# The recurrence's key tile without zero padding, multiplied as four 64x64 quarters

## The chip, the cores and the metric

One core of a Trainium2 chip runs the whole program. The metric is the device time of one execution in microseconds (us). The engines are TensorE (PE in the rows; PEld is its weight load), VectorE (DVE), ScalarE (ACT), GpSimd (POOL) and SyncE (SP), which here issues every DMA. Each takes its instructions in order from its own queue.

## The reference, cut to what matters

The program is one transformer layer on 2048 latent and 256 context tokens in float32: adaLN, a mixer of two head groups, and a gated MLP with a convolution. One head group is a bidirectional RWKV-7 recurrence of 8 heads of 64 channels, run forward and backward over the tokens:

```python
def step(S, inp):
    r_t, w_t, k_t, v_t, kk_t, b_t = inp
    sa = jnp.einsum('bhvk,bhk->bhv', S, kk_t)
    S = (S * w_t[:, :, None, :] - sa[..., None] * b_t[:, :, None, :]
         + v_t[..., None] * k_t[:, :, None, :])
    return S, jnp.einsum('bhvk,bhk->bhv', S, r_t)
```

The kernel computes it in chunks of 64 tokens. Inside a chunk the recurrence becomes products of the chunk's keys with its queries, the inverse of a triangular 64x64 matrix, and a few small matmuls that carry the state S from chunk to chunk.

## The kernel before

There are four phases, one after the other with some overlap: the input projection (phase 1, to about 945 us), the recurrence (phase 2b, about 945 to 1570 us), the attention of the other head group, and the output projection with the MLP.

**Phase 1** makes, besides other things, the key pairs of the recurrence. `prep` (40 calls: 4 head pairs, 5 blocks of tokens, 2 directions) builds a tile G of 128 partitions (two heads of 64 channels) by chunks by 128 columns. The columns of one chunk hold the two kinds of key, e = 0 and e = 1, of 64 tokens each. DVE finishes G (L530), and one DMA of SP (L531) stores it in the scratch tensor `pd`.

**Phase 2b** has 36 steps; step i handles one chunk of the forward and one of the backward direction (d = 0, 1), four head pairs each, so 8 units. Three pieces of work belong to it.

- `stage_g` (L1011 to L1035) multiplies keys by queries. `load` (L978) brings a 512 KB tile QP and the keys PK. PK has two halves: n = 0 holds the 64x64 blocks that stay on the block diagonal (head f, rows f and columns f), n = 1 those off it (rows f, columns 1-f), and the rest of both halves is zero, set once by POOL (L969). Four DMAs of 128 KB (L987) fill the blocks. For each d and n, L1018 makes four 128x128 matmuls into one PSUM bank `pa`. The n = 0 bank goes to AP by ACT (L1020), the n = 1 bank to ST by DVE in two half-height masked multiplies (L1026). POOL adds the two halves of PK to a dense tile PD (L1028, once per d), and PE transposes PD (L1033) for `tok`. ACT also copies QP into ST (L1024).
- `extract` and `invert`: ACT cuts the triangles out of AP (L1041), POOL masks them (L1042), and for two steps together (a pair) DVE transposes them (L1050), runs 31 rounds of two dependent small operations (L1056, L1057, 62 operations in all), and transposes the result twice (L1060, L1061).
- `assemble` and `chain`: the state update. PE forms Z (L1118), ACT copies the half of d = 0 and DVE that of d = 1 (L1120, Zk), PE multiplies by the inverse (L1133), ACT scales (L1135), PE multiplies by tok (L1142), DVE adds to the state S (L1143, once per d), and POOL scales it into X for the next step (L1146, L1147).

The three PSUM banks named `pa` rotate among L1018, L1033 and the two products of `assemble` (L1079, L1090). The order on each engine comes from a scheduler which weighs priorities that `boosted` sets for each piece; it interleaves several steps, and its order is what the order rows below show.

Of the kernel before, what the change touches and what calls it, by code (L numbers as in the profile page):

```python
# [8 lines left out]
F32 = mybir.dt.float32  # L9
# [3 lines left out]
ALU = mybir.AluOpType  # L13
# [4 lines left out]
P = 128  # L18
# [10 lines left out]
CH = 64  # L29
# [168 lines left out]
def phase1(tc, I, T, pr, ident, bones, keep):  # L198
    nc = tc.nc
    with ExitStack() as st:  # L200
# [3 lines left out]
        hp = rpool(st, "hT", 1)  # L204
# [101 lines left out]
        with ExitStack() as s2:  # L306
# [3 lines left out]
            pv = rpool(s2, "psv", 1, space=PSUM)  # L310
# [131 lines left out]
        with ExitStack() as s3:  # L442
# [50 lines left out]
            def prep(h, b, O, K):  # L493
                t0, n = BLOCKS[b]
                m = n // CH
                rr = K
                if b:
                    rr = cp.tile([P, BLK], F32, name="rr", bufs=2)
                    nc.sync.dma_start(out=rr, in_=T["rwT"][h * P:(h + 1) * P, t0:t0 + n])
                for d in range(2):  # L500
                    i0 = t0 // CH
                    if d:
                        i0 = 0 if b == 0 else 36 + 4 - i0 - m

                    def v(ap):
                        ap = ap[:, 0:n]
                        return ap[:, ::-1] if d else ap

                    def c(ap):
                        return ap[:, 0:n].rearrange("p (m t) -> p m t", t=CH)  # L510

                    t = []
                    for e in range(2):
                        z = pv.tile([P, BLK], F32, name="pk")
                        nc.tensor.matmul(z[:, 0:n], lhsT=W4[:, d, e, h * P:(h + 1) * P], rhs=los[b][:, e], start=True, stop=True)
                        t.append(cp.tile([P, BLK], F32, name="t%d" % e, bufs=2))
                        nc.scalar.activation(out=t[e][:, 0:n], in_=v(z), func=AF.Tanh, scale=0.5)
                    sg, ta = t
                    nc.gpsimd.tensor_scalar(out=sg[:, 0:n], in0=sg[:, 0:n], scalar1=0.5, scalar2=0.5, op0=ALU.mult, op1=ALU.add)
                    cs = cp.tile([P, BLK], F32, name="cs", bufs=2)  # L520
                    nc.vector.tensor_tensor_scan(out=cs[:, 0:n], data0=smask[:, 0:n], data1=sg[:, 0:n], initial=0.0, op0=ALU.mult, op1=ALU.add)
                    nc.scalar.activation(out=sg[:, 0:n], in_=cs[:, 0:n], func=AF.Exp, scale=-CDEC)
                    nc.scalar.activation(out=cs[:, 0:n], in_=cs[:, 0:n], func=AF.Exp, scale=CDEC)
                    W, IW = c(sg), c(cs)
                    nc.vector.tensor_copy(out=pr.wc[:, i0:i0 + m, d, h], in_=W[:, :, CH - 1])
                    G = cp.tile([P, 2 * BLK], F32, name="G", bufs=2)[:, 0:2 * n].rearrange("p (m e t) -> p m e t", e=2, t=CH)
                    nc.vector.scalar_tensor_tensor(out=G[:, :, 0], in0=c(ta), scalar=1.0, in1=c(v(K)), op0=ALU.add, op1=ALU.mult)
                    nc.scalar.activation(out=ta[:, 0:n], in_=ta[:, 0:n], func=AF.Identity, scale=hka[:, h:h + 1], bias=oka[:, h:h + 1])
                    nc.gpsimd.tensor_tensor(out=G[:, :, 1], in0=c(v(O)), in1=c(ta), op=ALU.mult)
                    nc.vector.tensor_tensor(out=G, in0=G, in1=IW.unsqueeze(2).broadcast_to([P, m, 2, CH]), op=ALU.mult)  # L530
                    nc.sync.dma_start(out=T["pd"][d * 4 + h, :, i0 * P:(i0 + m) * P], in_=G.rearrange("p m e t -> p (m e t)"))  # L531
                    Q = cp.tile([P, 2 * BLK], F32, name="Q", bufs=2)[:, 0:2 * n].rearrange("p (m t) -> p m t", t=P)
                    nc.gpsimd.tensor_tensor(out=Q[:, :, 1:CH], in0=c(v(K))[:, :, 1:CH], in1=W[:, :, 0:CH - 1], op=ALU.mult)
                    nc.scalar.copy(out=Q[:, :, 0:1], in_=c(v(K))[:, :, 0:1])
                    nc.gpsimd.tensor_tensor(out=Q[:, :, CH:P], in0=c(v(rr)), in1=W, op=ALU.mult)
                    nc.sync.dma_start(out=T["qd"][d * 4 + h, :, i0 * P:(i0 + m) * P], in_=Q.rearrange("p m t -> p (m t)"))
# [161 lines left out]
G = 3  # L698
# [243 lines left out]
CH = 64  # L942
# [4 lines left out]
def phase2b(tc, I, T, pr, ident):  # L947
# [17 lines left out]
        return ivx[1 if p >= 2 and p % 2 == 0 else 0]  # L965

    def pk_tiles(p, n):
        PK = p.tile([P, 2, 8, P], F32, name="PK%d" % n)
        nc.gpsimd.memset(PK, 0.0)  # L969
        PKs.append((p.tile([P, 8, P], F32, name="QP%d" % n), PK))  # L970

    order = [list(range(NS)), list(range(3, -1, -1)) + list(range(NS - 1, 3, -1))]
    bts, ivs, PKs = {}, [], []
    Ls, Bs = {}, {}
    qv = T["qd"].rearrange("u p (i t) -> i p u t", t=P)
    pv = T["pd"].rearrange("u p (i n t) -> i n p u t", n=2, t=CH)

    def load(i):  # L978
        if i >= NS or i in Ls:
            return  # L980
        QP, PK = PKs[1 if i >= 4 and i % 2 == 0 else 0]
        nc.sync.dma_start(out=QP, in_=qv[i])
        for n in range(2):
            for f in range(2):
                s = slice(f * 64, f * 64 + 64)
                o = (f ^ n) * 64
                nc.sync.dma_start(out=PK[s, n, :, o:o + 64], in_=pv[i, n, s])  # L987
        Ls[i] = QP, PK

    hd = lpool("rgen")  # L990
    gm = hd.tile([P, 2, P], F32, name="gm")
    adm = hd.tile([P, 32], F32, name="adm")
    PD = hd.tile([P, 8, P], F32, name="PD")
    pk_tiles(hd, 0)
    load(0)
    nc.sync.dma_start(out=gm, in_=I["gmask"].rearrange("p (a b) -> p a b", a=2))
# [11 lines left out]
    def psa():  # L1008
        return pam.tile([P, 4, P], F32, name="pa")

    def stage_g(i, B):  # L1011
        QP, PK = Ls.pop(i)
        for d in range(2):
            u = slice(d * 4, d * 4 + 4)
            for n in range(2):
                g = psa()
                for hp in range(4):
                    nc.tensor.matmul(g[:, hp], lhsT=PK[:, n, d * 4 + hp], rhs=QP[:, d * 4 + hp], start=True, stop=True)  # L1018
                if n == 0:
                    nc.scalar.copy(out=B["AP"][:, u], in_=g)  # L1020
                for f in range(2):
                    s, o = slice(f * 64, f * 64 + 64), slice((1 - f) * 64, (1 - f) * 64 + 64)
                    if n == 0:
                        nc.scalar.copy(out=B["ST"][s, u, f], in_=QP[s, u])  # L1024
                    else:
                        nc.vector.tensor_tensor(out=B["ST"][o, u, f], in0=g[o], in1=gm[o, 1:2].broadcast_to([64, 4, P]), op=ALU.mult)  # L1026
                yield
            nc.gpsimd.tensor_tensor(out=PD[:, u], in0=PK[:, 0, u], in1=PK[:, 1, u], op=ALU.add)  # L1028
        nc.gpsimd.tensor_tensor(out=B["AP"][:, :, CH:P], in0=B["AP"][:, :, CH:P], in1=gm[:, 1:2, CH:P].broadcast_to([P, 8, CH]), op=ALU.mult)
        for d in range(2):  # L1030
            g = psa()
            for hp in range(4):
                nc.tensor.transpose(out=g[:, hp], in_=PD[:, d * 4 + hp], identity=ident)  # L1033
            nc.scalar.copy(out=B["tok"][:, d * 4:d * 4 + 4], in_=g)
            yield  # L1035

# [843 lines left out]
```

## Time and profile before

| | |
|---|---|
| median of 3 runs | 4146.94 us |
| lowest, highest | 4144.19, 4151.88 us |
| span of the profiled execution | 4140.8 us |
| PE busy, share of span | 3824.6 us, 92% |
| DVE busy | 2671.8 us, 65% |
| ACT, POOL busy | 1881.5, 1543.3 us |

The span is that of the instructions in one profiled execution; the median lies 6.1 us above it. A share over the whole span mixes phases: outside the recurrence PE works on matmuls of 512 columns nearly without a gap, so the phase of the change has to be read by itself.

### The profile page before, as it was taken

Reading aid. Unit: us, or ns where it says so; the run is one execution under the profiler, and the core shown is the slowest. Engines: PE = TensorE matmul, PEld = TensorE weight load, DVE = VectorE, ACT = ScalarE, POOL = GpSimd, SP = SyncE. Lnnn points to the kernel's source line nnn. Section 1 sums busy time; section 2 is a strip of 40 time slices with the busy share of each in tenths; the row PEclk is TensorE's granted clock in tenths of the full one; section 3 lists DMA queues with packets and bytes.
Section 4 is the critical chain, followed back from the end, with each engine's and each line's share of the span. In section 5 each row is a group of like instructions: output and inputs, shape, how many; then the busy total and the mean of one; then the engine's idle time right before and its main releaser. Section 6 shows DMA issues by size and latency. Waiting matters only on the chain. (4 is left out here: it accounts for less than half of the span.)

```text
span 4140.8 us, 65493 instructions
## 1 busy us (share of the span) xinstructions
PE 3824.6 (92%) x25471; PEld 3213.6 (78%) x25471; DVE 2671.8 (65%) x3869; ACT 1881.5 (45%) x3678; POOL 1543.3 (37%) x1617
## 2 busy tenths in 40 slices
PE   7998888897899987989999899899999999999999
PEld 4777666676888876888898778788888888878887
DVE  3467678978889886888989868754444444420243
ACT  4235454466666656777777644521112112221211
POOL 3237467844444433455444366511101101022222
PEclk8999999998999988999999999999999999999999
DMA  4554546554434333020102163311111111131333
GB/s 174 160 168 154 162 146 214 205 161 94 97 95 101 94 85 101 8 61 22 33 6 74 51 219 136 117 61 51 46 43 62 46 41 56 51 101 44 115 114 102
DMA packets 464724, 400.80 MB, mean 97 GB/s; under 512 B 131613, under 2 KB 393702, under 8 KB 463390
## 3 DMA queue, kind: packets, MB, share of 16 engines
q1 hardware_dynamic: 464414, 396.61, 31.3%
q8 instruction: 201, 3.29, 0.3%
q14 instruction: 109, 0.89, 0.1%
HBM read 269.51 MB, written 131.74 MB: 97 GB/s over the span
## 5 line engine op out<-in xcount | busy, mean ns | idle before, releaser
L36 PE MATMUL o<-h2H,wuL 128*128 128x512 f32 x1920 | 761.7, 397 | 0.8 <-POOL wuL L1586 0.8
L34 PE MATMUL o<-h2H,wuH 128*128 128x512 f32 x1920 | 755.5, 394 | 5.6 <-DVE h2H L179 3.7
L35 PE MATMUL o<-h2L,wuH 128*128 128x512 f32 x1920 | 759.1, 395 | 0.2 <-DVE h2L L180 0.2
L1586 POOL TENSOR_TENSOR wuL<-wuraw,wuH 128x1024 fp32r<-128x1024 f32 x76 | 182.2, 2399 | 871.0 <-ACT wuH L1585 871.0
L34 PEld LDWEIGHTS o<-h2H,wuH 128*128 128x128 f32 x1920 | 362.0, 189 | 90.8 <-DVE h2H L179 3.9
L35 PEld LDWEIGHTS o<-h2L,wuH 128*128 128x128 f32 x1920 | 361.9, 189 | 89.9 <-DVE h2L L180 1.6
L36 PEld LDWEIGHTS o<-h2H,wuL 128*128 128x128 f32 x1920 | 362.1, 189 | 83.5 <-POOL wuL L1586 1.5
L34 PE MATMUL mm<-hH,wH 128*128 128x512 f32 (+1 forms) x968 | 384.5, 398 | 23.1 <-DVE hH L179 13.0
L787 DVE TENSOR_REDUCE nb<-S 128x1 f32<-128x768 f32 x384 | 357.8, 948 | 54.1 <-PE S L786 52.8
L35 PE MATMUL mm<-hL,wH 128*128 128x512 f32 (+1 forms) x968 | 382.0, 395 | 1.0 <-DVE rstd L162 0.9
L788 ACT ACTIVATE P<-S,nb 128x768 f32<-128x768 f32 x384 | 345.8, 907 | 77.4 <-DVE nb L787 74.5
L36 PE MATMUL mm<-hH,wL 128*128 128x512 f32 (+1 forms) x968 | 380.9, 394 | 0.0
L1617 DVE TENSOR_SCALAR co<-cs,cols 128x1024 f32<-128x1024 f32 x88 | 139.8, 1590 | 314.4 <-ACT cs L1606 313.0
L785 PE MATMUL S<-kH,qs 128*128 128x384 f32 x768 | 293.4, 382 | 36.1 <-ACT P L788 33.8
L829 PE MATMUL pv<-V,aT 128*128 128x128 f32 x2304 | 310.0, 279 | 5.5 <-DVE O L845 3.0
L1606 ACT COPY cs<-o 128x512 f32<-128x512 f32 x176 | 103.0, 586 | 449.8 <-PE o L36 449.6
L829 PEld LDWEIGHTS pv<-V,aT 128*128 128x128 f32 x2304 | 286.6, 195 | 9.1 <-DVE O L845 5.8
L786 PE MATMUL S<-kL,qs 128*128 128x384 f32 x768 | 261.2, 340 | 0.0
L815 DVE SCALAR_TENSOR_TENSOR P<-P,f,P 128x768 f32<-128x768 f32 x192 | 243.9, 1283 | 12.5 <-POOL P L813 10.9
L34 PEld LDWEIGHTS mm<-hH,wH 128*128 128x128 f32 x968 | 191.1, 198 | 63.8 <-DVE hH L179 13.9
L35 PEld LDWEIGHTS mm<-hL,wH 128*128 128x128 f32 x968 | 191.5, 198 | 40.2 <-DVE hL L180 2.2
L36 PEld LDWEIGHTS mm<-hH,wL 128*128 128x128 f32 x968 | 191.4, 198 | 38.9 <-issue 0.7
(362 smaller groups left out, 8103.6 us busy)
## 6 DMA issues: line engine op xcount, KB each, us to landing
wraw<-in_w_in_dram SPq DMA_DIRECT2D x52, 512.0 KB
wuraw<-in_w_up_dram SPq DMA_DIRECT2D x44, 512.0 KB
scr_actT<-co SPq DMA_DIRECT2D x44, 512.0 KB
QP<-scr_qd SPq DMA_DIRECT2D x36, 512.0 KB
PK<-scr_pd SPq DMA_DIRECT2D x144, 128.0 KB
mww<-in_w_mod_dram SPq DMA_DIRECT2D x64, 256.0 KB
scr_pd<-G SPq DMA_DIRECT2D x32, 512.0 KB
scr_qd<-Q SPq DMA_DIRECT2D x32, 512.0 KB
```

The lines of the kernel that those rows point to most:

```text
L34: nc.tensor.matmul(out, lhsT=lH, rhs=rH, start=first, stop=False)
L35: nc.tensor.matmul(out, lhsT=lH, rhs=rL, start=False, stop=False)
L36: nc.tensor.matmul(out, lhsT=lL, rhs=rH, start=False, stop=last)
L785: nc.tensor.matmul(S[:, b, 0:HB], lhsT=qs[:, qt * P:(qt + 1) * P], rhs=kH[:, sl], start=True, stop=False)
L786: nc.tensor.matmul(S[:, b, 0:HB], lhsT=qs[:, qt * P:(qt + 1) * P], rhs=kL[:, sl], start=False, stop=True)
L787: nc.vector.tensor_reduce(out=nb[:, m, g:g + 1], in_=S[:, :, 0:HB], op=ALU.max, axis=AX.XY, negate=True)
L788: nc.scalar.activation(out=Pm[m][:, g * GW:(g + 1) * GW].rearrange("p (b x) -> p b x", b=2), in_=S[:, :, 0:HB], func=AF.Exp, bias=nb[:, m, ...
L815: nc.vector.scalar_tensor_tensor(out=Pm[0][:, sls[g - 1]], in0=Pm[0][:, sls[g - 1]], scalar=f[:, 0, g - 1:g], in1=Pm[1][:, sls[g - 1]], op ...
L829: nc.tensor.matmul(pv, lhsT=aT[:, j], rhs=V[:, k0 + j], start=(k0 + j == 0), stop=(k0 + j == KTT - 1))
L1586: eng.tensor_tensor(out=L, in0=raw, in1=H.bitcast(F32), op=ALU.subtract)
L1606: nc.scalar.copy(out=S[:, 1 + b * BLK:1 + (b + 1) * BLK], in_=o)
L1617: nc.vector.tensor_scalar(out=O, in0=S[:, t0:t0 + 1024], scalar1=w[0], scalar2=None, op0=ALU.mult)
```

## The change

The keys are stored so that one 128x128 tile per unit is already what PD was. `prep` writes the partitions of head 0 as they are and those of head 1 with the two kinds of key exchanged, so one DMA becomes three. `load` brings PK with one DMA. PK has no zero half and no memset; PD and its POOL addition are gone, and the transposes read PK. Each 128x128 product of n = 0 and n = 1 becomes two 64x64 quarters (64 rows, 64 columns of weights, 128 columns moving); the diagonal ones write bank `g`, the others bank `go`, both asked for at once.

```diff
-                    nc.sync.dma_start(out=T["pd"][d * 4 + h, :, i0 * P:(i0 + m) * P], in_=G.rearrange("p m e t -> p (m e t)"))
+                    pdst = T["pd"][d * 4 + h, :, i0 * P:(i0 + m) * P].rearrange("p (m e t) -> p m e t", e=2, t=CH)
+                    nc.sync.dma_start(out=pdst[0:64], in_=G[0:64])
+                    for e in range(2):
+                        nc.sync.dma_start(out=pdst[64:128, :, 1 - e], in_=G[64:128, :, e])
...
-        PK = p.tile([P, 2, 8, P], F32, name="PK%d" % n)
-        nc.gpsimd.memset(PK, 0.0)
-        PKs.append((p.tile([P, 8, P], F32, name="QP%d" % n), PK))
+        PKs.append((p.tile([P, 8, P], F32, name="QP%d" % n), p.tile([P, 8, P], F32, name="PK%d" % n)))
...
-        for n in range(2):
-            for f in range(2):
-                s = slice(f * 64, f * 64 + 64)
-                o = (f ^ n) * 64
-                nc.sync.dma_start(out=PK[s, n, :, o:o + 64], in_=pv[i, n, s])
+        nc.sync.dma_start(out=PK, in_=pv[i])
...
-            for n in range(2):
-                g = psa()
-                for hp in range(4):
-                    nc.tensor.matmul(g[:, hp], lhsT=PK[:, n, d * 4 + hp], rhs=QP[:, d * 4 + hp], start=True, stop=True)
-                if n == 0:
-                    nc.scalar.copy(out=B["AP"][:, u], in_=g)
+            g, go = psa(), psa()
+            for hp in range(4):
                 for f in range(2):
-                    s, o = slice(f * 64, f * 64 + 64), slice((1 - f) * 64, (1 - f) * 64 + 64)
-                    if n == 0:
-                        nc.scalar.copy(out=B["ST"][s, u, f], in_=QP[s, u])
-                    else:
-                        nc.vector.tensor_tensor(out=B["ST"][o, u, f], in0=g[o], in1=gm[o, 1:2].broadcast_to([64, 4, P]), op=ALU.mult)
-                yield
-            nc.gpsimd.tensor_tensor(out=PD[:, u], in0=PK[:, 0, u], in1=PK[:, 1, u], op=ALU.add)
+                    nc.tensor.matmul(g[HF[f], hp], lhsT=PK[HF[f], d * 4 + hp, HF[f]], rhs=QP[HF[f], d * 4 + hp], start=True, stop=True)
+                    nc.tensor.matmul(go[HF[1 - f], hp], lhsT=PK[HF[f], d * 4 + hp, HF[1 - f]], rhs=QP[HF[f], d * 4 + hp], start=True, stop=True)
+            nc.scalar.copy(out=B["AP"][:, u], in_=g)
+            for f in range(2):
+                nc.scalar.copy(out=B["ST"][HF[f], u, f], in_=QP[HF[f], u])
+            yield
+            for f in range(2):
+                o = HF[1 - f]
+                nc.vector.tensor_tensor(out=B["ST"][o, u, f], in0=go[o], in1=gm[o, 1:2].broadcast_to([64, 4, P]), op=ALU.mult)
+            yield
...
-                nc.tensor.transpose(out=g[:, hp], in_=PD[:, d * 4 + hp], identity=ident)
+                nc.tensor.transpose(out=g[:, hp], in_=PK[:, d * 4 + hp], identity=ident)
```

The scheduler orders the queues anew. In the changed kernel the lines of the recurrence are numbered differently: L1015 and L1016 are the products into `g` and `go` (L1018 before), L1023 the masked multiply into ST (L1026), L1029 the transposes (L1033), L1114 and L1121 the products of Z and of the output (L1118, L1125), L1116 Zk (L1120), L1139 the state (L1143), L1046 the transpose that begins an inversion (L1050), L1052 and L1053 its 62 operations (L1056, L1057), L1056 and L1057 its closing transposes (L1060, L1061).

On DVE, where one pair's inversion ends. The kernel before has two inversions in flight there: Tt1 ends while Tt0 already runs.

```order
L1056 TENSOR_TENSOR tmp1_7621<-X_1_7620,Tt0_6647 128x56
L1057 TENSOR_TENSOR Tt1_6656<-Tt1_6656,tmp0_6640 128x3x15
L1057 TENSOR_TENSOR Tt0_6647<-Tt0_6647,tmp1_7621 128x28x2
L1143 TENSOR_TENSOR S0_7615<-pc_11711,S0_7615 128x256
L1056 TENSOR_TENSOR tmp0_6640<-X_0_6639,Tt1_6656 128x30
L1056 TENSOR_TENSOR tmp1_7621<-X_1_7620,Tt0_6647 128x81
L1057 TENSOR_TENSOR Tt1_6656<-Tt1_6656,tmp0_6640 128x2x15
L1057 TENSOR_TENSOR Tt0_6647<-Tt0_6647,tmp1_7621 128x27x3
L1056 TENSOR_TENSOR tmp0_6640<-X_0_6639,Tt1_6656 128x16
L1056 TENSOR_TENSOR tmp1_7621<-X_1_7620,Tt0_6647 128x78
```

The changed kernel, at the same kind of place in the sixth pair:

```order
L1053 TENSOR_TENSOR Tt1_6731<-Tt1_6731,tmp0_6715 128x16
L1056 STREAM_TRANSPOSE D1_6732<-Tt1_6731 128x32x16
L1057 STREAM_TRANSPOSE Dt1_6733<-D1_6732 128x512
L1023 TENSOR_TENSOR ST2_6725<-pa_9670,gm_6644 64x4x128 x2
L1116 COPY Zk1_9658<-pc_9649 128x256
L1139 TENSOR_TENSOR S0_7730<-pc_9781,S0_7730 128x256
L1139 TENSOR_TENSOR S1_7732<-pc_9821,S1_7732 128x256
L1023 TENSOR_TENSOR ST3_6728<-pa_9909,gm_6644 64x4x128 x2
L1046 STREAM_TRANSPOSE X_1_7735<-AD1_7734 128x32x32
L1023 TENSOR_TENSOR ST3_6728<-pa_9963,gm_6644 64x4x128 x2
L1052 TENSOR_TENSOR tmp1_7736<-X_1_7735,Tt0_6722 128x31
```

An inversion now begins only after the one before it has ended, at all of the turns, and the chain's Zk, S0 and S1 stand between the two without an operation of an inversion among them.

On PE, the second direction's keys times queries in the kernel before, with the counters that each instruction waits for:

```order
L1018 MATMUL pa_13347<-QP1_7588,PK1_7586 128x128 [waits Activation_49]
L1018 MATMUL pa_13347<-QP1_7588,PK1_7586 128x128 x3
L1018 MATMUL pa_13355<-QP1_7588,PK1_7586 128x128 [waits DVE_49,PE_49]
L1018 MATMUL pa_13355<-QP1_7588,PK1_7586 128x128 x3
L1133 MATMUL pc_13370<-Zk0_13278,Tb0_7611 64x64 [waits Activation_49]
```

The changed kernel there:

```order
L1015 MATMUL pa_12209<-QP1_7708,PK1_7709 64x128 [waits PE_49]
L1015 MATMUL pa_12209<-QP1_7708,PK1_7709 64x128 x7
L1114 MATMUL pc_12124<-X00_7714,ST3_6728 64x64 [waits DMAHW0_49,PE_49,Pool_49]
L1114 MATMUL pc_12124<-X00_7714,ST3_6728 64x64 x3
L1016 MATMUL pa_12210<-QP1_7708,PK1_7709 64x128 [waits Activation_49]
L1016 MATMUL pa_12210<-QP1_7708,PK1_7709 64x128 x7
L1029 MATMUL pa_12252<-ident_75,PK1_7709 128x128 [waits DVE_49,PE_49]
L1029 MATMUL pa_12252<-ident_75,PK1_7709 128x128 x3
L1114 MATMUL pc_12124<-X00_7714,ST3_6728 64x64 [waits DMAHW1_49,Pool_49]
```

The eight products into `g` stand together and those into `go` after them, because `go` has to wait for a free bank; only in the first direction do the two alternate. The transposes moved ahead of the rest of the chain's Z product and wait for DVE, which empties the first direction's `go` bank.

## Rows read from the trace of the kernel before

**Rows 1.** Stretches: span of each, busy us of each engine (instructions), granted clock, DMA share, GB/s.

```profile
310.00:840.00 530.00, 446.93 (x2052) 361.00 (x2051) 422.41 (x433) 263.69 (x495) 354.55 (x265) 0.92 0.54 177
945.00:1510.00 565.00, 500.94 (x8030) 446.14 (x8031) 498.10 (x1221) 374.37 (x848) 259.43 (x316) 0.92 0.40 94
```

**Rows 2.** L1143 (DVE, S): count, shortest/median/longest ns, first and last start.

```profile
L1143 DVE TENSOR_TENSOR S<-pc,S x70: 383/418/426, 966.6 to 1569.4; 128x256 f32<-128x256 f32 x70
```

**Rows 3.** Groups of 950 to 1520: form, count | busy us, mean ns | idle before, releaser.

```profile
L1018 PE MATMUL pa<-QP,PK 128*128 128x128 f32 x1022 | 143.7, 293 | 2.0 <-ACT AP L1020 1.9
L1026 DVE TENSOR_TENSOR ST<-pa,gm 64x512 f32<-64x512 f32 x128 | 88.1, 688 | 18.5 <-PE pa L1018 16.4
L1028 POOL TENSOR_TENSOR PD<-PK 128x512 f32<-128x512 f32 x64 | 82.3, 1298 | 8.3 <-DMA PK<-scr_pd 7.5 <-PE pa L1033 0.6
```

**Rows 4.** Waits of PE, 960 to 1500: waiter, releaser, us in total, times, longest.

```profile
PE pc L1133 <- DVE Zk L1120: 39.7, 14, 3.9
```

**Rows 5.** Waits of DVE, same stretch.

```profile
DVE S L1143 <- PE pc L1142: 26.6, 26, 3.3
DVE ST L1026 <- PE pa L1018: 16.4, 23, 2.6
```

**Rows 6.** POOL in order of time: start, us, line, operation, count, [idle before].

```profile
1316.58 1.32 POOL L1028 TENSOR_TENSOR PD<-PK 128x512 f32<-128x512 f32 x1
...
1318.60 1.32 POOL L1028 TENSOR_TENSOR PD<-PK 128x512 f32<-128x512 f32 x1
```

**Rows 7.** DVE in order of time, beside rows 6.

```profile
1315.52 1.39 DVE L1026 TENSOR_TENSOR ST<-pa,gm 64x512 f32<-64x512 f32 x2 [0.34 <-PE pa L1018]
1316.84 1.21 DVE L1057 TENSOR_TENSOR Tt<-Tt,tmp 128x126 f32<-128x126 f32 x1
...
1318.82 1.25 DVE L1057 TENSOR_TENSOR Tt<-Tt,tmp 128x136 f32<-128x136 f32 x1
1320.10 0.29 DVE L1056 TENSOR_TENSOR tmp<-X,Tt 128x128 f32<-128x128 f32 x1
```

**Rows 8.** DVE in order of time, an earlier stretch.

```profile
1301.03 0.44 DVE L1056 TENSOR_TENSOR tmp<-X,Tt 128x31 f32<-128x31 f32 x2
...
1302.88 0.30 DVE L1057 TENSOR_TENSOR Tt<-Tt,tmp 128x56 f32<-128x56 f32 x2
...
1309.47 0.26 DVE L1056 TENSOR_TENSOR tmp<-X,Tt 128x96 f32<-128x96 f32 x1
1309.76 0.26 DVE L1057 TENSOR_TENSOR Tt<-Tt,tmp 128x96 f32<-128x96 f32 x1
```

**Rows 9.** PE in order of time.

```profile
1301.29 0.68 PE L1133 MATMUL pc<-Zk,Tb 64*64 64x64 f32 x16 [2.94 <-DVE Zk L1120]
...
1307.77 0.22 PE L1118 MATMUL pc<-X,ST 128*64 128x64 f32 x1
1307.77 0.22 PE L1125 MATMUL py<-ST,X 128*64 128x64 f32 x1
...
1309.36 2.05 PE L1018 MATMUL pa<-QP,PK 128*128 128x128 f32 x16
```

**Rows 10.** Stretches after one wait of PE, columns as in rows 1.

```profile
1300.00:1307.00 7.00, 5.71 (x81) 5.08 (x82) 5.88 (x25) 2.84 (x8) 1.51 (x3) 0.76 0.23 59
1307.00:1335.00 28.00, 25.97 (x448) 23.13 (x448) 26.27 (x53) 20.91 (x47) 14.87 (x18) 1.00 0.47 110
```

**Rows 11.** DMA issues of SP: ns shortest/median/longest; last, idle of the engine that writes G.

```profile
L987 SPq DMA_DIRECT2D PK<-scr_pd x144: 582/626/1742, 537.7 to 1471.7; - x144
L531 SPq DMA_DIRECT2D scr_pd<-G x40: 319/320/1240, 321.3 to 841.4; - x40
...
  DMA scr_pd<-G: 1.8, 2
```

**Rows 12.** DMA queue 1 in 960 to 1500: packets, MB, share of 16 engines.

```profile
q1 hardware_dynamic: 142244, 49.88, 38.9%
```

More of the change, by code (lines that the diff above doesn't have):

```diff
@@ L975, in phase2b @@
     qv = T["qd"].rearrange("u p (i t) -> i p u t", t=P)
-    pv = T["pd"].rearrange("u p (i n t) -> i n p u t", n=2, t=CH)
+    pv = T["pd"].rearrange("u p (i t) -> i p u t", t=P)
+    HF = [slice(f * 64, f * 64 + 64) for f in range(2)]
     def load(i):
@@ L992, in phase2b @@
     adm = hd.tile([P, 32], F32, name="adm")
-    PD = hd.tile([P, 8, P], F32, name="PD")
     pk_tiles(hd, 0)
```

## The prediction

> **What bounds the kernel now.** I read the windows by stage first. In the recurrence, 945 to 1510 us, PE is busy 500.9 of 565 us and DVE 498.1, at a granted clock of 0.92 [rows 1]. Two engines at 88% cannot both be the end all the time, so the next views are the waits of each. PE waits 39.7 us for DVE's Zk, in 14 pieces of about 3 us [rows 4]. DVE waits for PE in 26 + 23 short pieces, 26.6 us for the state's product and 16.4 us for the product that goes into ST [rows 5]. So DVE sets the end for long runs of instructions and PE for short ones. The state's addition shows the pace: 70 of them from 966.6 to 1569.4 us, two per step, are 34 steps of 17.7 us, or 17 pairs of steps of 35.5 us [rows 2]. A pair is the right unit, because one inversion (62 small dependent operations on DVE) serves two steps.
>
> The group view names what the change touches: the products L1018, 143.7 us of PE; the masked multiply L1026, 88.1 us of DVE; the addition PD, 82.3 us of POOL in 64 instructions of 1.30 us [rows 3].
>
> **PD is removed.** POOL is not the bound, but its addition is felt on DVE. While PD runs (1316.58 to 1317.90, and again from 1318.60), the inversion's operation beside it takes 1.21 and 1.25 us and ends 0.15 us after PD; the operation that comes next, alone, takes 0.29 us [rows 6, 7]. L1026, which reads PSUM, is not stretched: its mean over 128 is 0.69 us, the same as two that stand where no PD runs (1.39 us) [rows 3, 7]. So one PD that meets an operation between SBUF tiles costs DVE about 0.95 us. Following the 64 through the trace, three of four meet one: 48 x 0.95 = 45 us. Bounds: nothing, if DVE is not the end where they fall, and 61 us if all met one. I take **-45**, since most fall in stretches in which DVE is without a gap. POOL's other work stays.
>
> **The inversions lose their overlap.** Before, two inversions are in flight where one pair ends and the next begins. There 16 operations take from 1301.03 to 1303.18 us, 0.134 us each, while in a serial stretch one follows the other at 0.29 us [rows 8]: the second chain fills the time in which the first waits for its own result. The order of the changed kernel has no such stretch at any of the 17 turns. At 14 of them the old order has one of about 16 operations: 14 x 16 x 0.155 = **+35**. Lower end 0, where DVE has to wait at the turn anyway; upper end 17 turns, 42.
>
> **The turns.** At 7 turns of the new order the chain's Zk, S0 and S1 and the masked multiplies stand on DVE with no operation of an inversion between them; in the old order I find 3 such places. There DVE waits for PE's round trip: for S and for ST. Such a wait now is 1.0 and 0.7 us in the mean, 3.3 and 2.6 us at its longest [rows 5], so a turn costs 1.7 to 5.9 us. I take the middle, 3.8, since several of them follow each other there: 4 more turns are **+15** (bounds 7 and 24).
>
> **Between the turns** the new order is kinder: S and ST stand behind runs of inversion operations, 0.29 us each, so PE has time to finish. Half of the 43 us that DVE waits now [rows 5] is covered: **-20** (0 to -43).
>
> **The transposes** L1029 now wait for DVE, which must empty the first direction's `go` bank, and stand ahead of the rest of the chain's Z product on PE. Queued behind them are Z, hence Zk on DVE and ACT, the inverse's product and S. Before, L1018 waits nearly nowhere (2.0 us in all) [rows 3]. The nearest row for a PE wait on DVE is 39.7 / 14 = 2.8 us [rows 4]. DVE has inversion operations to do meanwhile, so most of it is covered; what comes back to DVE lies between 0 and what it waits for ST today, 16.4 us [rows 5]. I take **+10**, since nearly every step has one.
>
> **The clock.** After a wait of PE of 2.94 us [rows 9] the window 1300 to 1307 has a granted clock of 0.76, the next 28 us 1.00 [rows 10], that is, PE drops from 2.4 to 1.2 GHz for a while. 7 x 0.24 = 1.7 us of PE are lost each time. The new order has some 8 more such waits (4 turns and as many of the transposes that come at a bad moment): 8 x 1.7 = **+14** (0 to 24).
>
> **The products.** Now 8 matmuls of 128x128, 16 records, take 2.05 us there [rows 9], 0.11 to 0.13 us a record. The change has 16 matmuls of 64x64 per direction. If only the two on a diagonal run at once (as L1133's do: 16 records in 0.68 us for 64 columns moving [rows 9]), 16 matmuls take what 8 took. In the first direction the four quarters alternate and could run four at once, half of 1.8 us saved per step; if none ran together it would be 1.8 us more per step. In 34 steps that is -31 to +61 us of PE. In the second direction the order asks for all of `g`, then all of `go`: pairs on a diagonal, no change. L1118 and L1125, which use the same rows and the two halves of the columns, begin at the same hundredth of a microsecond [rows 9], so products with the same rows do run together. I take **0**: PE's gain in one direction shortens no wait of DVE that the terms above don't count.
>
> Here a page speaks against the change. The Trainium skill, "TensorE: Matmul & The Clock Gate", Part 3, section "The mechanism", says that a weight load overlaps running matmuls only where the row groups differ. By that rule neighbours with the same rows would load one after the other; the pair in rows 9 speaks against it. What no row shows is two products with the same columns and different rows at once.
>
> **Phase 1 and the loads.** L531's one DMA (0.32 us of SP) becomes three. The two short ones have 256-byte pieces like those of L987, issued in 0.63 us [rows 11]: 2 x 0.63 x 40 = 50 us of SP, spread over 530 us, in a phase where the wait for a store of G is 1.8 us in all [rows 11]. They add 36,864 pieces. A packet takes 0.389 x 540 x 16 / 142,244 = 0.0236 us [rows 12], so 54 us of 16 engines' time, estimated from that row, at a share of 0.54 now [rows 1]. I price it at +5: that wait a little more than doubled, and the same again for other loads queued behind it; bounds 0 to 20. In the recurrence, four DMAs of PK become one, with fewer pieces; they were off the path, and without the memsets the first load comes earlier: -3. Together **+2**.
>
> **Sum.** -45 + 35 + 15 - 20 + 10 + 14 + 2 = +11. The profiled span is 4140.8 us, so 4151.8 after; the median lies 6.1 us above the span, so **4158 us**.
>
> **The rivals.** *DVE alone sets the end (faster).* PD's removal is kept whole, and the round trips at the turns hide, because PE runs ahead by then: -45 + 35 - 20 + 2 = -28, or 4119 us. For it: DVE without a gap over most of the phase, and only 43 us of waits. Against it: PE is as busy, and no operation stands between Zk and S at the turns. Chance 0.27.
>
> *The waits come but the clock holds (no change).* The turns and the transposes cost what I say, but PE is given other steps' products to do, so no granted clock falls: -28 + 15 + 10 = -3, or 4144 us. For it: the clock is 1.00 over 28 us in which PE is busy 93% [rows 10]. Against it: the new waits are of the kind after which it did fall. Chance 0.23.
>
> *The quarters run one at a time (slower).* In the first direction 16 matmuls then take 3.6 us instead of 1.8: 61 us more of PE. It decides as soon as that exceeds PE's idle time in the phase, 64 us [rows 1], in a given step; taking half as absorbed, +30 on the forecast: 4188 us. A milder form is that the change does not do what it says: in the second direction it never has four quarters at once; that alone is in the sum at nothing. The page named above would lead to this case. Against it: the start times in rows 9. Chance 0.14.
>
> **How the numbers follow.** The forecast has 0.36, with a range of its own from 4148 to 4172. A difference of 0.2%, 8.3 us, is about what a measurement of this kernel can tell from no change, so faster means below 4138.6 and slower above 4155.2. Faster: the first rival and a little of the second, 0.30. Same: the rest of the second and the low end of the forecast, 0.28. Slower: the forecast's upper part and the third rival, 0.42. The range goes from 4112, below the first rival, to 4190, just above the third; what is left out is the case that PD gives its upper bound with no lost overlap, and serial quarters that nothing absorbs.
>
> **What would show it.** Right: in the profile after, no inversion operation above 0.9 us where PD stood; inversion operations at about 0.29 us apart throughout; new waits of PE's L1029 for DVE's L1023 and of DVE's S and Z at the turns; more stretches with a clock below 0.9; a pair of steps near 36 us. The first rival is right if pairs fall to 34 us with DVE busy throughout. The third is right if the group L1015 takes 3.6 us per direction. It would be wrong altogether if phase 1 moved by more than 10 us, or if DVE's operations stay stretched under POOL's remaining work, so that removing PD gives less than half of its 45 us.

## The result, and the profile after

The changed kernel took 4178.76 us (4174.19 to 4188.74, 4 runs), the kernel before 4145.56 us beside it. The ratio is 1.0081, with an interval from 1.0063 to 1.0099: 34 us slower. The forecast was 4158 us, in a range from 4112 to 4190. The sign came as forecast, the size is about three times as large.

The windows, with columns as in [rows 1], and the state's additions, as in [rows 2], of the kernel after:

```profile
310.00:840.00 530.00, 454.46 (x2094) 368.95 (x2092) 412.24 (x434) 265.26 (x497) 357.76 (x263) 0.91 0.63 177
945.00:1510.00 565.00, 435.62 (x8430) 375.76 (x8432) 448.89 (x1153) 354.84 (x794) 165.49 (x235) 0.84 0.33 90
```

```profile
L1139 DVE TENSOR_TENSOR S<-pc,S x70: 409/418/426, 964.0 to 1628.0; 128x256 f32<-128x256 f32 x70
```

Phase 1 is where it was: the DMA share went from 0.54 to 0.63 (the 54 us of the estimate would make 0.64), and the first addition to the state comes 2.6 us earlier. The recurrence goes from 964.0 to 1628.0 us, 664 us instead of 603. The phases that follow give some of the 59 us back: the attention's first reduction comes 52 us later than before, its last 40, and the end 35. Why they are shorter was not followed up.

So the loss is in the recurrence. There every engine is busy for less time than before, in the same 565 us, in which fewer steps now fit: PE 436 instead of 501, DVE 449 instead of 498, and the granted clock is 0.84 instead of 0.92. The group rows, with columns as in [rows 3]:

```profile
L1016 PE MATMUL pa<-QP,PK 64*64 64x128 f32 x964 | 91.2, 306 | 40.3 <-ACT AP L1017 40.3
L1029 PE MATMUL pa<-ident,PK 128*128 128x128 f32 x240 | 55.8, 375 | 63.8 <-DVE ST L1023 37.9 <-DVE tmp L1052 24.9 <-ACT AP L1017 1.0
L1046 DVE STREAM_TRANSPOSE X<-AD 128x1024 f32<-128x1024 f32 x15 | 31.6, 2105 | 43.5 <-POOL AD L1038 43.5
```

L1016, L1029 and L1046 have 40, 64 and 44 us of idle time ahead of them. Before, L1018 had 2.0 us in all [rows 3], the transposes 0.4 and the beginning of an inversion 0.0:

```profile
L1033 PE MATMUL pa<-ident,PD 128*128 128x128 f32 x256 | 41.6, 288 | 0.4 <-ACT AP L1020 0.4
L1050 DVE STREAM_TRANSPOSE X<-AD 128x1024 f32<-128x1024 f32 x16 | 32.5, 2034 | 0.0
```

The waits of PE and of DVE in the changed kernel, as in [rows 4, 5]:

```profile
PE pa L1029 <- DVE ST L1023: 37.9, 11, 8.5
PE pa L1016 <- ACT AP L1017: 35.5, 7, 6.1
PE pa L1029 <- DVE tmp L1052: 24.9, 3, 8.7
PE pc L1129 <- DVE Zk L1116: 15.2, 7, 3.8
```

```profile
DVE X L1046 <- POOL AD L1038: 40.3, 14, 3.1
DVE S L1139 <- PE pc L1138: 32.2, 17, 4.7
DVE ST L1023 <- PE pa L1015: 5.8, 5, 1.3
```

PE's one large wait, 39.7 us for Zk [rows 4], is down to 15.2, but 98 us of others have come. On DVE the wait for ST fell from 16.4 to 5.8 us, as forecast; the wait for S rose from 26.6 to 32.2; and the beginning of an inversion waits 40 us for its input, a wait that the trace of before didn't have. A wait of PE is not yet a loss: banks_in_turn, further down, has nearly the same ones and is 37 us faster. One turn of a pair shows how they hang together (start, us, engine, line, operation, and in brackets the idle time and what ended it):

```profile
1354.45 1.06 DVE L1056 STREAM_TRANSPOSE D<-Tt 128x512 f32<-128x512 f32 x1
...
1355.54 1.64 ACT L1080 COPY Tb<-D 32x256 f32<-32x256 f32 x4 [4.57 <-DVE D L1056]
1357.21 1.07 ACT L1017 COPY AP<-pa 128x512 f32<-128x512 f32 x2
...
1357.85 1.97 PE L1016 MATMUL pa<-QP,PK 64*64 64x128 f32 x16 [5.15 <-ACT AP L1017]
...
1360.04 0.72 POOL L1038 TENSOR_TENSOR AD<-AD,adm 128x256 f32<-128x256 f32 x1 [0.41 <-ACT AD L1037]
...
1360.80 2.10 DVE L1046 STREAM_TRANSPOSE X<-AD 128x1024 f32<-128x1024 f32 x1 [3.13 <-POOL AD L1038]
```

DVE ends an inversion. ACT's copies of it into Tb have stood in ACT's queue for 4.57 us, and behind them stand the copies into AP, whose bank PE needs: PE waits 5.15 us. The copies into AP give AD, by POOL, and only then can DVE begin the next inversion: it has waited 3.13 us. PE, POOL and DVE wait one after the other behind ACT. A transpose that waits for DVE to empty the bank `go` holds PE for longer still, at its longest 8.47 us, while 14 operations of an inversion and an addition to the state stand ahead of ST on DVE:

```profile
1307.21 1.09 PE L1029 MATMUL pa<-ident,PK 128*128 128x128 f32 x4 [8.47 <-DVE ST L1023]
```

**The matmuls are not the loss.** Where the order leaves the first direction in one piece, as in the steps just ahead of the first addition to the state, the four quarters start within 0.02 us of each other; 32 records last from 891.02 to 892.12 us:

```profile
891.02 0.32 PE L1015 MATMUL pa<-QP,PK 64*64 64x128 f32 x1
891.02 0.32 PE L1016 MATMUL pa<-QP,PK 64*64 64x128 f32 x1
891.03 0.32 PE L1015 MATMUL pa<-QP,PK 64*64 64x128 f32 x1
891.04 0.32 PE L1016 MATMUL pa<-QP,PK 64*64 64x128 f32 x1
...
891.85 0.27 PE L1016 MATMUL pa<-QP,PK 64*64 64x128 f32 x1
```

In the second direction, where all products of `g` stand ahead of those of `go`, 16 records take as long by themselves:

```profile
1321.55 1.09 PE L1016 MATMUL pa<-QP,PK 64*64 64x128 f32 x16
```

That is 1.10 us for 16 matmuls in one direction and 2 x 1.09 us in the other, where 8 full matmuls took 2.05 us [rows 9]. PE's own work could so fall by 0.8 us a step. Inside the recurrence it doesn't: there the first direction is taken apart and stands among the chain's products (in the step that begins at 1345.56 us its 32 records are spread over 5.7 us), and from 950 to 1520 us the products take 4.1 us of PE a step (124.4 us for 1928 records, overlaps counted once, at the lower clock) where they took 4.5 (143.7 us for 1022 records [rows 3]). That little buys nothing.

### The profile page after: what moved, and what is told of

It reads as the page before. It is cut to its first block, busy times and chain, and to the rows that moved or that the text cites. A ratio compares the mean times of both kernels' runs of the same rounds, so it can differ in the third digit from the quotient of the medians.

```text
span 4175.4 us, 67605 instructions
## 1 busy us (share of the span) xinstructions
PE 3808.7 (91%) x26623; PEld 3181.6 (76%) x26623; DVE 2632.9 (63%) x3869; ACT 1885.5 (45%) x3678; POOL 1455.2 (35%) x1543
## 5 line engine op out<-in xcount | busy, mean ns | idle before, releaser
L1142 POOL TENSOR_TENSOR X<-S,wc 64x256 f32<-64x256 f32 x140 | 85.5, 611 | 424.3 <-DVE S L1139 385.5
```

## The experiments

Times are medians in us; the ratio is to runs of the kernel before on the same chip, and the last column is that ratio times 4145.6 us.

| run | us | ratio, interval | us against before |
|---|---|---|---|
| the change | 4178.8 | 1.0081 (1.0063 to 1.0099) | +34 |
| pd_by_dma | 4106.2 | 0.9904 (0.9888 to 0.9919) | -40 |
| quarters_alone | 4187.8 | 1.0102 (1.0087 to 1.0117) | +42 |
| quarters_pd_by_dma | 4156.0 | 1.0013 (1.0000 to 1.0027) | +5 |
| banks_in_turn | 4142.1 | 0.9992 (0.9982 to 1.0001) | -3 |
| pd_back | 4205.4 | 1.0153 (1.0127 to 1.0179) | +63 |
| store_alone | 4171.0 | 1.0066 (1.0051 to 1.0081) | +27 |
| dense_store | 4120.5 | 0.9939 (0.9924 to 0.9953) | -25 |
| t_on_dve | 4215.8 | 1.0177 (1.0155 to 1.0198) | +73 |
| transposes_late | 4219.5 | 1.0175 (1.0152 to 1.0198) | +73 |
| transposes_first | 4232.0 | 1.0213 (1.0195 to 1.0231) | +88 |
| overlap_in_turn | 4130.9 | 0.9962 (0.9950 to 0.9974) | -16 |
| overlap_both_banks | 4159.9 | 1.0038 (1.0023 to 1.0052) | +16 |

### What is POOL's addition worth?

**pd_by_dma**, the kernel before with PD loaded (into two buffers) and not added:

```diff
+                nc.sync.dma_start(out=PD[s, :, o:o + 64], in_=pv[i, n, s])
...
-            nc.gpsimd.tensor_tensor(out=PD[:, u], in0=PK[:, 0, u], in1=PK[:, 1, u], op=ALU.add)
```

> The kernel before, with one change: POOL no longer adds the halves of PK into PD; four more DMAs of SP per step load a dense PD (two buffers). Matmuls, banks and layout stay as they were, and the inversions still overlap in the order of DVE. Theory 'order' (removing the addition is worth what the prediction says, and the loss of the changed kernel comes from the new order of the queues): 30 to 45 us faster than before, 4100 to 4117 us. Rival 'no gain' (DVE has slack where the addition stretches it, so its removal is worth little): 4138 to 4150 us. Rival 'loads' (more pieces of 256 bytes cost time by themselves): slower than 4150 us.

Measured: 40 us faster, and this is the fastest kernel of the study. The gain can be read directly. The operations of the inversions in the recurrence (line, forms, count, busy us, mean ns, idle before), of the kernel before, then of pd_by_dma:

```profile
L1056 DVE TENSOR_TENSOR tmp<-X,Tt 128x126 f32<-128x126 f32 (+22 forms) x496 | 182.5, 380 | 9.2
L1057 DVE TENSOR_TENSOR Tt<-Tt,tmp 128x126 f32<-128x126 f32 (+22 forms) x496 | 173.6, 362 | 9.1
```

```profile
L1059 DVE TENSOR_TENSOR tmp<-X,Tt 128x126 f32<-128x126 f32 (+21 forms) x496 | 150.8, 315 | 9.6
L1060 DVE TENSOR_TENSOR Tt<-Tt,tmp 128x126 f32<-128x126 f32 (+21 forms) x496 | 167.5, 349 | 9.3
```

356 us became 318: 38 us, with the same 992 operations. The inversions overlap at the turns as before, and DVE's idle time in the recurrence stays where it was (86.5 us of 602.8 before, 82.5 of 563.1 here; columns as in [rows 1]):

```profile
969.20:1532.30 563.10, 514.84 (x8710) 460.01 (x8706) 480.57 (x1275) 385.62 (x878) 189.25 (x266) 0.93 0.58 127
```

**pd_back** asks the same from the other side, the changed kernel with an addition on POOL that the transposes read:

```diff
+            nc.gpsimd.tensor_tensor(out=PD[:, u], in0=PK[:, u], in1=zr.broadcast_to([P, 4, P]), op=ALU.add)
...
-                nc.tensor.transpose(out=g[:, hp], in_=PK[:, d * 4 + hp], identity=ident)
+                nc.tensor.transpose(out=g[:, hp], in_=PD[:, d * 4 + hp], identity=ident)
```

> The changed kernel, with POOL's addition put back: it copies PK into PD (PK plus a tile of zeros, 128x512, two per step) and the transposes read PD. The order of DVE is the same as in the changed kernel. Theory 'order': the stretched operations cost again, less than 45 us because DVE now has some 100 us of waits in which a part is hidden: 4190 to 4224 us. Rival 'no gain': within 8 us of the changed kernel, 4171 to 4187 us.

Measured: 30 us slower than the changed kernel. The operations take 318 us in the changed kernel and 342 us in pd_back:

```profile
L1052 DVE TENSOR_TENSOR tmp<-X,Tt 128x126 f32<-128x126 f32 (+22 forms) x496 | 159.8, 322 | 15.0
L1053 DVE TENSOR_TENSOR Tt<-Tt,tmp 128x126 f32<-128x126 f32 (+22 forms) x496 | 158.2, 319 | 14.7
```

```profile
L1056 DVE TENSOR_TENSOR tmp<-X,Tt 128x126 f32<-128x126 f32 (+22 forms) x496 | 176.1, 355 | 15.0
L1057 DVE TENSOR_TENSOR Tt<-Tt,tmp 128x126 f32<-128x126 f32 (+22 forms) x496 | 165.7, 334 | 14.8
```

So the addition costs about what it stretches (38 us for 40 of time, and 24 us for 30), in an order with few waits on DVE and in one with many. Both times lie where 'order' had them. "No gain" falls.

### Which part of the change loses?

**quarters_alone**, the kernel before with its products as quarters:

```diff
-                    nc.tensor.matmul(g[:, hp], lhsT=PK[:, n, d * 4 + hp], rhs=QP[:, d * 4 + hp], start=True, stop=True)
+                    for f in range(2):
+                        s, o = slice(f * 64, f * 64 + 64), slice((f ^ n) * 64, (f ^ n) * 64 + 64)
+                        nc.tensor.matmul(g[o, hp], lhsT=PK[s, n, d * 4 + hp, o], rhs=QP[s, d * 4 + hp], start=True, stop=True)
```

> The kernel before, with only the products changed: each 128x128 matmul of the padded tile becomes two 64x64 quarters; layout, loads, banks one after the other, and POOL's addition stay. By its order the inversions overlap at 3 turns instead of 17. Theory 'order': the quarters' number alone changes the order, so the loss is here without the gain of PD: 30 to 80 us slower than before, 4175 to 4225 us. Rival 'layout' (the loss is that of the stored layout and its DMAs): 4138 to 4155 us. Rival 'no gain': the transposes that no longer wait for POOL are what costs, and they still wait here: 4138 to 4160 us.

Measured: 42 us slower, where 'order' had it, with layout, loads and the order of banks as before. By records the quarters take PE no longer than the full matmuls (123.9 us for 1928 records from 950 to 1520 us, 4.1 us a step); what changed with their number is the order that the scheduler makes. The inversions overlap at one turn where they did at 14. DVE is busy 9 us longer in the recurrence and idle 39 us longer (125.5 us instead of 86.5):

```profile
974.10:1624.30 650.20, 505.78 (x9690) 447.64 (x9689) 524.72 (x1280) 389.27 (x883) 262.86 (x328) 0.82 0.36 89
```

PE now waits for DVE at places where it didn't (L1035 are the transposes, L1092 a product of `assemble`):

```profile
PE pa L1035 <- DVE ST L1028: 31.5, 10, 7.8
PE pa L1092 <- DVE ST L1028: 23.6, 3, 8.5
```

No run puts the quarters into the old order; that the order is the whole of the 42 us is argued from these rows.

**quarters_pd_by_dma** makes both edits in the kernel before.

> Both edits of pd_by_dma and quarters_alone in the kernel before: quarters, banks in turn, the old layout, and a dense PD loaded by four DMAs instead of POOL's addition. If the two add up: 42 us slower for the quarters, 38 us faster without the addition, 4149 us, between 4143 and 4156 us; against banks_in_turn (4142 us) the rest is then the new layout with its single load, some 7 us to its credit. Rival (with the order of the quarters DVE has waits in which the stretched operations were hidden, so the addition is worth less): 4160 us or more. Rival (the four more DMAs of pd_by_dma hide a larger gain): no prediction of its own here, since they are in both.

Measured: 5 us slower than before, by medians 8, with 4156.0 us at the edge of the range in which the two add up; +42 and -40 do so to within what can be measured.

**banks_in_turn**, the changed kernel, but `go` is asked for after `g` has been filled and handed on:

```diff
-            g, go = psa(), psa()
+            g = psa()
...
+            yield
+            go = psa()
```

> The changed kernel, but the bank g is asked for, filled and given to ACT before the bank go is asked for, as the kernel before does; all quarters are then pairs on a diagonal. It differs from quarters_alone only by the missing addition PD and the layout. Theory 'order': what quarters_alone measured (43 us slower) less 27 to 38 us for PD, 4150 to 4165 us. Rival (asking for both banks at once is the loss): 4125 us or less, near the gain of pd_by_dma.

Measured: 3 us faster than before, 37 us faster than the changed kernel. Both expectations missed: it lies between them. Against quarters_pd_by_dma, 9 us (by the intervals some 2 to 16) are to the credit of the layout with its single load and no memsets. Its waits of DVE for AD and for S in 960 to 1500 are small again:

```profile
DVE X L1049 <- POOL AD L1041: 6.7, 7, 1.2
DVE S L1142 <- PE pc L1141: 9.6, 10, 4.0
```

Its waits of PE are not (L1023 are the products into `go`, L1032 the transposes):

```profile
PE pa L1023 <- ACT AP L1016: 33.9, 8, 5.1
PE pa L1032 <- DVE ST L1026: 33.5, 13, 7.5
PE pa L1032 <- DVE tmp L1055: 19.8, 2, 10.0
```

87 us of the kind of which the changed kernel has 98, in a kernel that is as fast as the one before. So of the changed kernel's new waits, those that go with its 37 us are DVE's and not PE's: for AD and S banks_in_turn waits 34 and 23 us less, for ST 19 more (25.0 us).

With these runs the change comes apart into four steps: the quarters +42, the missing addition -37, layout and load -9, both banks at once +37. The third is counted within these kernels; by itself the stored layout costs time (below). Each run differs from the next by one step, so the sum is bound to be that of the change; what it tells is that two losses, both of order as far as the rows show, ate a gain that is there.

### Is it one wait?

**t_on_dve** moves the copies that ACT's queue waits with:

```diff
-            nc.scalar.copy(out=Tc[s, :, (g % 2) * 32:(g % 2) * 32 + 32], in_=D[s])
+            nc.vector.tensor_copy(out=Tc[s, :, (g % 2) * 32:(g % 2) * 32 + 32], in_=D[s])
```

> The changed kernel, with the four copies of the inverse into Tb (L1080) moved from ACT to DVE, which made the inverse and so never waits for it. Theory 'order', in the form that ACT's queue waits there for DVE with the copies into AP and AD standing behind (ACT waits 40 us for D, then DVE 44 us for AD): both waits go below 15 us, 144 copies of about 0.3 us come to DVE, in all 10 to 30 us faster than the changed kernel, 4149 to 4169 us. Rival (those waits only stand where something else is late anyway): 4171 us or more.

Measured: 40 us slower than the changed kernel, as the rival had it. The waits that the edit aimed at did shrink (the inversion's for AD from 44 to 19 us in the whole recurrence), and DVE's idle time there fell from 160 to 132 us. But DVE is busy for 562 us instead of 504, 39 us of it the copies themselves:

```profile
967.40:1661.80 694.40, 523.51 (x9668) 452.21 (x9664) 561.97 (x1411) 341.71 (x748) 186.83 (x269) 0.80 0.30 83
```

So this run puts more work on DVE than it saves in waits, and does not tell what ACT's queue costs. PE's transposes wait 110 us for DVE in 960 to 1500, 63 in the changed kernel:

```profile
PE pa L1029 <- DVE ST L1023: 75.7, 15, 7.0
PE pa L1029 <- DVE tmp L1052: 34.5, 4, 9.0
```

**transposes_late** puts the transposes into a piece of their own with a lower priority (4500 became 2500); **transposes_first** puts them ahead of the products:

```diff
+        yield from boosted(toks(i, Bs[i]), 'K', i)
```

> The changed kernel, with the transposes in a piece of their own that has a lower priority: on PE they now stand behind the inverse's product and not directly behind the product into go. Theory, in the form that PE's transposes which wait for DVE's evacuation of go are the largest single loss (65 us of PE waits): these waits go below 20 us and the time falls by 20 to 45 us, 4134 to 4159 us. Rival (another wait takes their place, since the inversions still don't overlap): 4160 to 4190 us.

```diff
         QP, PK = Ls.pop(i)
+        for d in range(2):
+            g = psa()
+            for hp in range(4):
+                nc.tensor.transpose(out=g[:, hp], in_=PK[:, d * 4 + hp], identity=ident)
```

> The changed kernel, with the transposes ahead of the products g and go in each step, so that they wait only for PK and for banks that ACT empties. Theory as for transposes_late: the transposes' waits for DVE go, 4134 to 4159 us. Rival: the wait for DVE moves to the products that need the bank next, and the time stays within 10 us of the changed kernel, 4169 to 4189 us.

Measured: 39 and 55 us slower than the changed kernel, beyond the ranges of the theory and of both rivals. In both the transposes stopped waiting for DVE (5 us left in the first), and something else waits longer. In the first it is the inverse's product, for DVE's Zk, up to 12.5 us at a time; in the second the first product of `assemble`, for the inversion:

```profile
PE pc L1134 <- DVE Zk L1121: 125.3, 13, 12.5
PE pa L1033 <- DVE ST L1024: 5.4, 2, 4.5
```

```profile
PE pa L1075 <- DVE Tt L1053: 47.8, 6, 9.8
```

My theory in the form "the transposes are the loss", which I expected to win back 20 to 45 us, is wrong; banks_in_turn, in which they wait 53 us and nothing is lost, says the same. The form with ACT's queue stays open. In these two runs the wait that was taken out came back elsewhere, since the scheduler orders everything anew.

### Is it the lost overlap?

**overlap_in_turn** and **overlap_both_banks** hold an inversion's last 16 operations back until the next one has begun, in banks_in_turn and in the changed kernel:

```diff
+        if pending:
+            with tc.issue_after(nc.cur_bb.bb.instructions[-1]):
+                finish(*pending.pop())
```

> The run banks_in_turn, with the overlap of the inversions put back by hand: the last 16 operations of an inversion and its closing transposes are held back until the transpose that begins the next one has been issued, so the two chains alternate on DVE at 16 turns. Everything else is left to the order. My term for the overlap: 16 operations at 0.155 us saved, 2.5 us a turn, 35 to 42 us faster than banks_in_turn, 4100 to 4107 us. Rival (the overlap is a sign of an order in which DVE has no waits, not its cause; holding operations back adds waits for S and ST): 4130 us or more.

> The changed kernel with the same edit: the last 16 operations of an inversion wait in the queue behind the beginning of the next. Theory (the lost overlap is a loss of its own): 30 to 42 us faster than the changed kernel, 4137 to 4149 us. Rival (the waits of PE for DVE with both banks asked for at once stay, and the overlap only shifts them): 4165 us or more.

Measured: 12 us faster than banks_in_turn and 18 us faster than the changed kernel, a third to a half of what I had priced. Both theories missed; the first run lands where its rival begins, the second short of its rival. The recurrence of banks_in_turn, then of overlap_in_turn, as windows from the first to the last addition to the state:

```profile
972.90:1583.90 611.00, 484.66 (x9686) 427.28 (x9684) 495.78 (x1279) 391.02 (x884) 188.70 (x269) 0.87 0.35 94
```

```profile
972.90:1573.10 600.20, 505.71 (x9730) 449.61 (x9725) 443.52 (x1276) 388.95 (x886) 189.68 (x269) 0.87 0.34 94
```

The overlap does what I said for DVE's work: busy time falls from 496 to 444 us, 52 us, more than my 35. But DVE's idle time rises from 115 to 157 us. When the work on DVE shrinks in this order, the waits for PE take most of it: the one for S is 63.0 us in 960 to 1500, 9.6 in banks_in_turn. The edit also brings the end of each inversion later, and what that costs was not separated from what the overlap gives, so 12 to 18 us are the worth of this edit and not a price of the overlap.

### What does the stored layout cost?

**dense_store** is pd_by_dma with the new layout, **store_alone** the kernel before with it:

```diff
-                nc.sync.dma_start(out=PK[s, n, :, o:o + 64], in_=pv[i, n, s])
+                nc.sync.dma_start(out=PK[s, n, :, o:o + 64], in_=pv[i, s, :, o:o + 64])
```

> The run pd_by_dma with the changed kernel's stored layout: phase 1 stores G by three DMAs, and a step loads PK's halves by four DMAs and the dense PD by one. Matmuls as in the kernel before, order nearly that of pd_by_dma. Theory 'order' (the layout and its DMAs cost nothing that can be measured, as the start of the recurrence in the changed kernel suggests, 2.6 us earlier): within 8 us of pd_by_dma, 4098 to 4114 us. Rival 'layout' (256-byte stores cost time in phase 1): 4116 us or more.

> The kernel before, with the changed kernel's stored layout alone: phase 1 stores G by three DMAs and the four loads of PK read from that layout; POOL adds PD and the matmuls are as before. It asks what the 14 us between dense_store and pd_by_dma were. If the stores cost them: 4155 to 4162 us. If they came with that kernel's order at the start of the recurrence: 4138 to 4152 us, and the recurrence starts within 4 us of the kernel before.

Measured: 14 us slower than pd_by_dma, as the rival had it, and 27 us slower than before, more than either expectation. The layout is not free. In dense_store the first addition to the state comes 11 us later than in pd_by_dma (980.0 and 969.2 us). In store_alone G waits 9.2 us for its stores instead of 1.8, its last store is issued 17 us later than before, and the first addition to the state comes 26 us later, at 992.2 us (the trace is that of its slowest run, 4180.5 us; the others took 4168.0 to 4171.8):

```profile
L534 SPq DMA_DIRECT2D scr_pd<-G x80: 583/624/1516, 324.2 to 859.3; - x80
...
  DMA scr_pd<-G: 9.2, 4
```

In the changed kernel the last store is issued 2 us later and the state begins 2.6 us earlier. What makes up for the stores there may be what it has besides, no memsets and one load of PK per step instead of four, or the order: with the same stores and loads the state begins at 972.9 us in banks_in_turn and at 963.0 in overlap_both_banks. These were not separated, and where the rest of the 26 us arises in store_alone was not followed; that stays open.

## Why the prediction was right in sign and short in size

The forecast for the recurrence by itself was +9 us (-45 + 35 + 15 - 20 + 10 + 14); measured are +61. A pair of steps takes 39.1 us, where 36 was named as the sign of being right. By the spans 2.6 us of this came back ahead of the recurrence and 24 behind it, and for the 24 the prediction had no term. So that the time lies in the range is in part luck.

- **PD, -45.** Right in kind, somewhat large: 38 us by the records, 40 by the clock (pd_by_dma). Two counts make it up, and both are off: from 950 to 1520 us 57 of the 64 additions, not 48, meet an operation that takes over 0.9 us, and each costs 0.7 us and not 0.95. The two L1026 of [rows 7] do meet an addition, in their last 0.33 us; the reading from them holds all the same, since over the trace the 28 that meet one for more than 0.3 us take 0.687 us and the 108 that meet none 0.689.
- **Lost overlap, +35.** The order lost it at all turns, as read: in the trace of the changed kernel no operation of an inversion starts before the one ahead has ended, where the kernel before has 17 or more at 14 turns. As DVE's time the size was right. Against pd_by_dma, which lacks the addition too and keeps the overlap, DVE is busy for 504 us instead of 481, and idle for 29.7 us instead of 18.9 between the inversions' operations. What it cost the kernel is not shown; the edit that puts it back gives 12 to 18 us.
- **The waits of DVE at and between the turns, +15 and -20.** This is the step that failed. The wait for ST did fall, as forecast (18.4 to 9.3 us over the recurrence), and the one for S rose by 17, about as the turns had it. But the wait of an inversion's beginning for AD, 43.5 us, had no term at all. The order showed it: AP's copies stood behind Tb's on ACT. I read DVE's and PE's rows of the order and not ACT's.
- **Transposes +10, clock +14.** The waits came (63 us for the transposes), and the granted clock of the recurrence fell from 0.91 to 0.82, so the second rival is out. How much each of them cost can't be told: banks_in_turn has 53 us of the same waits and a clock of 0.87 in a recurrence of 611 us.
- **The sum of the waits** can be read in one pair of windows over the recurrence, of the kernel before and after, with the additions to the state in them:

```profile
966.60:1569.40 602.80, 530.85 (x8698) 472.99 (x8698) 516.26 (x1276) 387.85 (x882) 264.06 (x327) 0.91 0.39 93
L1143 DVE TENSOR_TENSOR S<-pc,S 128x256 f32<-128x256 f32 x69 | 28.8, 418 | 28.4 <-PE pc L1142 28.2 <-issue 0.2
```

```profile
964.00:1628.00 664.00, 521.64 (x9688) 448.70 (x9690) 504.14 (x1279) 396.04 (x888) 187.93 (x269) 0.82 0.32 88
L1139 DVE TENSOR_TENSOR S<-pc,S 128x256 f32<-128x256 f32 x69 | 28.9, 419 | 45.6 <-PE pc L1138 44.2 <-POOL X L1142 1.4
```

DVE's busy time fell from 516 to 504 us (36 us less with the addition gone, as in pd_by_dma, and 24 more without the overlap), its idle time rose from 87 to 160. That +73, less 12, is the 61 us by which the recurrence grew. Of the +73, 43.5 are the wait for AD, 17 that for S, -9 that for ST, 11 the gaps between the inversions' operations that the overlap had filled, and 10 the rest. My terms for waits (+15, -20, +10, +14) come to +19.

- **The products, 0.** Right for the time. The four quarters do run at once, so the third rival is out. The Trainium skill, "TensorE: Matmul & The Clock Gate", Part 3, "The mechanism", has weight loads overlap running matmuls only between different row groups. Here pairs with the same rows start 0.00 to 0.01 us apart, and with the same columns 0.01 to 0.02 us apart, so the trace decides against it for these tiles.
- **Phase 1 and the loads, +2.** The net was right (-2.6 us at the start of the recurrence), the parts were not: the stores alone cost 14 to 27 us, not 5. What gives them back in the changed kernel stays open, and since that start moves by 10 us between kernels with the same stores and loads, the net is in part luck.
- **The first rival** needed DVE to stay the end after the change. In pd_by_dma, where the order stays nearly as it was, the addition's worth is kept whole. (Its 4106 us lie near the rival's 4119, but that sum has a lost overlap and shorter waits in it, which this run has not.) In the changed kernel the order was no longer one in which DVE had work at hand.

## What to carry to other kernels

A change that alters the number of instructions on one engine lets a scheduler order all engines anew, and here two such steps cost 79 us while the removed work gave 37; read the order of every engine that hands on a buffer, ACT too, for copies that are ready but stand behind one that waits. Price a wait by the chain that comes after it (87 us of PE's waits went with no loss in banks_in_turn), and a saving on an engine only as far as that engine has something else to do. To win the gain of one part, make that part alone: taking the addition off POOL and leaving the matmuls as they were is 40 us faster than before.

## What the runs showed of the hardware

Sixteen 64x64 fp32 matmuls of 128 columns, four quarters issued in turn, took 1.10 us; the same number issued as two sets of diagonal pairs took 2 x 1.09 us; so which quarters stand next to each other in the queue decides whether two or four run at once. And POOL's 128x512 addition between SBUF tiles, 64 times 1.3 us, cost DVE's small SBUF operations 38 us in a nearly unchanged order, nearly half of its own time, and left the multiplies that read PSUM as they were (0.687 us beside it, 0.689 without).
